# Dilated stage: ScalarE's conversions of weights and values kept behind the instruction written ahead of them, and two groups' weight loads issued by SyncE

## Chip, core and metric

The kernel runs on one core of one Trainium2 chip. The metric is the device time of one execution in microseconds; lower is better. Times are given as the median of several runs, and one further execution is recorded by the hardware profiler. All views shown here come from that one.

## What is computed

The kernel computes a trunk of two layers over 1024 tokens of width 1024: layer 0 mixes tokens by latent attention, layer 1 by dilated sliding-window attention, and each is followed by an MLP. The change touches the dilated attention alone:

```python
DIL_GROUPS = ((128, 1), (512, 4), (2048, 16))   # window, dilation
DIL_HEADS = 16
DIL_HEAD_DIM = 64

def dilated_mixer(h, pos, w_in, g_q, g_k, rel_bias, w_o):
    B, S, _ = h.shape
    proj = (h @ w_in).reshape(B, S, N_DIL_GROUPS, 3, DIL_HEADS, DIL_HEAD_DIM)
    outs, lses = [], []
    for gi, (window, dilation) in enumerate(DIL_GROUPS):
        q = rms_norm(proj[:, :, gi, 0], g_q[gi])
        k = rms_norm(proj[:, :, gi, 1], g_k[gi])
        v = proj[:, :, gi, 2]
        table = rel_bias[:, gi * DIL_HEADS:(gi + 1) * DIL_HEADS]
        o, lse = dilated_group(q, k, v, pos, table, window, dilation)
        outs.append(o)
        lses.append(lse)
    o_all = jnp.stack(outs, axis=0)
    wts = jax.nn.softmax(jnp.stack(lses, axis=0), axis=0)
    o = jnp.einsum('gbsh,gbshd->bshd', wts.astype(o_all.dtype), o_all)
    return o.reshape(B, S, DIL_HEADS * DIL_HEAD_DIM) @ w_o
```

Within a group, a query sees the keys of its own residue class within the window, with a bias by relative position; the three groups' outputs are merged by their softmax denominators.

## The kernel before

**Numbers in two parts.** A matrix product in float32 precision is made of three products of shorter numbers. Each operand is split into a high part (a ScalarE copy into the shorter type, line 121) and a low part (operand minus high part, line 122, mostly on VectorE); lines 414 to 416 multiply high by high, high by low and low by high. Values of v are split into three bf16 parts (lines 1815 to 1818), probabilities into two fp16 parts (lines 1923 and 1924).

**Steps of the dilated stage.** The values v of all groups are already projected and lie in HBM when `dil` (line 1749) starts; q and k are projected in it. It runs over a list of steps (line 2046): for each of the three groups 8 head pairs, for each pair 4 steps of two token tiles. Between two groups stands one step without a projection, in which the activations are permuted into the next group's token order (`permute`, line 2077: copies on ScalarE, VectorE and GpSimd); it begins already in the step before. Here these are called the turns. Group 0 fills the trace from 1669 to about 1953 us, group 1 from about 1987 to 2233, group 2 from about 2284 to 2552.

**One step n** writes, in this order:

- `fetch(n + 2)` (line 2054): if a head pair begins two steps on, its weights' loads, `dil_weights` (line 1542): two raw tiles `wqkr` of 512 KB, two DMAs of 256 KB each, issued by ScalarE;
- the parts of v that are due (`vtodo`, line 2063): for every second pair, which starts at step m, the loads `v_load` (SyncE) at step m − 4, and from step m − 2 on one call of `v_parts` in each step, five or four in all (line 1815 on ScalarE, 1816 on VectorE, 1817 and 1818 on GpSimd);
- at a turn, the permuting copies;
- `fetch_split(n + 1)` (line 2058): if a head pair begins at the next step, its weights' conversions, for each of the two raw tiles a high part `wqkh` on ScalarE and a low part `wqkl` on VectorE;
- `attend` (line 1898) for two earlier query tiles: the score products `pss` (line 1869), then for each tile the bias load `bt` (SyncE, line 1878), bias and row maximum (VectorE, 1883), the exponent's offset `dnb` and the exponentials (ScalarE, 1887 and 1889) and the two parts `ph` of the probabilities; then one DMA transpose `pT` of both (SyncE, line 1925);
- half of the projection `psproj`, the PE transposes `psq` of an earlier step (line 1844) with the split into `kT` (1848 and 1849), the other half of the projection;
- `av` (line 1928): the products `psav` with v of the tiles whose probabilities were transposed a step before;
- `qkstep` (line 1822): squares `dsq`, sums `dms`, the normalisation (line 112, Ln `drl`, and line 113, Exp `dry`, on ScalarE, then VectorE), and the scaled `qn`.

**What sets the order.** The program is not run as written. A planner, given the written program, puts each engine's instructions in an order of its own: with a modelled time for each, it lets an engine take the first written instruction whose inputs and buffer are there. So an instruction that depends on little, such as a load or a conversion of weights, can come out much earlier than it is written. On the chip every engine then runs its own list strictly in that order, and an instruction whose input is late holds up all that follow it in that list; DMA issues stand in the list of the engine that issues them. Two things bind the planner: `pinned` (line 203) keeps instructions of an engine in the order written, and `pin_from` (line 193) adds a dependence of each instruction on its engine's predecessor, without a wait on the chip, since one engine runs in order anyway. `pin_from` is used for TensorE in the dilated stage (line 2172), so there TensorE's order is the one written; ScalarE, VectorE, GpSimd and SyncE are the planner's.

**Buffers.** Weight tiles, raw values, merged outputs and permuted activations share one pool of 29 tiles (line 47); the planner gives a tile to a load when one is free. The converted values `vs` have 8 buffers of their own, the probabilities `ph` and `pT` two each, the bias tiles three.

Of the kernel before, what the change touches and what calls it, by code (L numbers as in the profile page):

```python
# [14 lines left out]
AF = mybir.ActivationFunctionType  # L15
# [26 lines left out]
class K:  # L42
# [150 lines left out]
    def pin_from(self, mark, engine=None):  # L193

        bb = self.nc.cur_bb.bb.instructions
        last = {}
        for n, i in enumerate(bb):
            prev, last[i.engine] = last.get(i.engine), i
            if n >= mark and prev is not None and engine in (None, i.engine):
                self.tc.add_manual_dep(i, prev.name, mybir.DependencyInfo(  # L200
                    mybir.DependencyClass.NoSync, mybir.DependencyReason.DATA), reason="pin_from")

    def pinned(self, ins):
        return self.tc.keep_in_program_order(ins)
# [1544 lines left out]
    def dil(self, at0, at1, tail, wqk, vd):  # L1749


        nc, a, tc = self.nc, self.a, self.tc
# [54 lines left out]
        def v_parts(raws, VS, t):  # L1807

            n = min(2, (9 if len(raws) == 3 else 8) - t)
            vs = D_("vs", (P, 2, 4, 192), BF16, 8)  # L1810
            p4 = raws[t // 4][:, t % 4 : t % 4 + n].rearrange("p i (h e) -> p (i h) e", e=64)
            v4 = vs[:, 0:n].rearrange("p i h e -> p (i h) e")
            r = self.T("vr")
            r4 = r.rearrange("p (i e) -> p i e", e=64)[:, 0 : 4 * n]
            nc.scalar.activation(v4[:, :, 0:64], p4, AF.Copy)
            nc.vector.tensor_tensor(r4, p4, v4[:, :, 0:64], op=ALU.subtract)
            nc.gpsimd.tensor_scalar(v4[:, :, 64:128], r4, 1.0, 1.0, op0=ALU.mult, op1=ALU.mult)
            nc.gpsimd.tensor_tensor(v4[:, :, 128:192], r4, v4[:, :, 64:128], op=ALU.subtract)
            for i in range(n):
                VS[t + i] = vs[:, i]  # L1820
# [195 lines left out]
        def emit(u, ths):  # L2016

            pr = u["pr"]
            if pr == 6:
                for k in range(2):  # L2020
                    for th in range(2):
                        O[k][th][3] = self.G(f"oT{k}", (P, 2, 512))
            for th in ths:
                ps = PS("psot")
                for i in range(4):
                    nc.tensor.transpose(ps[:, i * P : (i + 1) * P], u["U"][:, 4 * th + i, :], self.ident)
                if pr >= 6:
                    self.split(O[0][th][3][:, pr - 6, :], O[1][th][3][:, pr - 6, :], ps)
                else:
                    s_ = self.G("oT", (P, 2, 512))  # L2030
                    self.split(s_[:, 0, :], s_[:, 1, :], ps)
                    nc.scalar.dma_start(out=oTd[pr, th], in_=s_.bitcast(F32))
# [16 lines left out]
        loads, wts = {}, {}  # L2049
        mark = len(nc.cur_bb.bb.instructions)  # L2050
        end = max(n for n, x in enumerate(steps) if x is not None)
        firsts = {n: s for n, s in enumerate(steps) if s is not None and s[3] == 0}

        def fetch(n):
            if n in firsts:
                loads[n] = self.dil_weights(*firsts[n][1:3], eng=nc.scalar)

        def fetch_split(n):
            if n in firsts:
                wts[firsts[n][0:3]] = loads.pop(n)()  # L2060


        vtodo, VSs = {}, {}
        for n, (_, g, pr, _) in firsts.items():
            if pr % 2 == 0:
                VS = VSs[(g, pr // 2)] = {}
                VS["load"] = lambda g=g, c=pr // 2, VS=VS: VS.update(raws=v_load(g, c))
                vtodo.setdefault(n - 4, []).append(VS["load"])
                for t in range(0, 9 if g < 2 else 8, 2):
                    vtodo.setdefault(n - 2 + t // 2, []).append(lambda t=t, VS=VS: v_parts(VS["raws"], VS, t))  # L2070
                vtodo.setdefault(n - 2 + t // 2, []).append(lambda VS=VS: VS.pop("raws"))
# [35 lines left out]
        for n in sorted(vtodo):  # L2107
            if n < 0:
                for f in vtodo.pop(n):
                    f()  # L2110
        for n, step in enumerate(steps):
            fetch(n + 2)
            for f in vtodo.pop(n, ()):
                f()
# [11 lines left out]
            if step is not None:  # L2126
                kind, g, pr, tp = step
                w = wts[(kind, g, pr)]
                if tp == 0:
                    units[(g, pr)] = {"g": g, "pr": pr, "q": {}, "V": VSs[(g, pr // 2)],  # L2130
                                      "k": D_("kT", (P, 2, S + 512), F32R, 2), "U": self.G("U", (P, 8, P), F32)}
                u = units[(g, pr)]
            fetch_split(n + 1)
            transposed, scored = scored, attend(ready, n > end) if ready else []
            for u_, t_, _ in scored:
# [11 lines left out]
            if len(stk) > 1:  # L2147
                x = stk.pop(0)
# [200 lines left out]
```

## Time and profile before

| | |
|---|---|
| median of 3 runs | 3287.01 us (3286.89 to 3298.17) |
| the profiled execution | 3286.91 us |
| its span, from first to last instruction | 3285.1 us |
| mean granted TensorE clock | 0.983 |
| stretch 1660 to 2600 us, the dilated stage | 940 us |
| weight loads from ScalarE's queue | 92 DMAs of 256 KB |
| weight loads from SyncE's queue | 4 DMAs, written ahead of the stage |
| DMA transposes `pT` | 95 |

How to read the rows that follow. A row of busy time by stretch has the stretch, its length, then for TensorE's matmuls (PE), its weight loads into the array (PEld), VectorE (DVE), ScalarE (ACT) and GpSimd (POOL) the busy time and in parentheses the number of instructions, then the mean granted TensorE clock, the mean busy share of the 16 DMA engines and GB/s. That share can pass 1 in a short stretch, since a packet counts where it starts. A row of waits has the waiting instruction, what ended its wait, the total, how often, and the longest, in us. A row of the timeline has start, duration, engine (with a q where it is the queue that issues), line, operation, what is written and read, shape, count, and in brackets the engine's idle time ahead of it with what ended that. A row of groups has line, operation, shapes, count, then busy time, mean duration in ns, idle time ahead and what ended it. A row of the chain of waits has start and duration.

### The profile page before, as it was taken

What the parts mean: (1) busy time and instruction counts of PE and PEld (TensorE: products, weight loads), DVE (VectorE), ACT (ScalarE), POOL (GpSimd) and SP (SyncE); (2) the same over time, 40 slices, a digit from 0 to 9 for tenths busy, and PEclk for the clock granted to TensorE, in tenths of its full rate; (3) what the DMA queues carried; (4) which work ended last, traced back from release to release, by engine and by line L of the source; (5) the groups of instructions that cost most, each with busy time, mean ns of one, the idle gap of its engine ahead of it and who ended that gap; (6) DMA issues with size and microseconds to landing.
All of it is one profiled execution on the core that took longest, in us unless ns stands there. A gap on an engine that the chain in (4) does not pass through costs nothing. (4 is left out here: it accounts for less than half of the span.)

```text
span 3285.1 us, 50852 instructions
## 1 busy us (share of the span) xinstructions
PE 3143.2 (96%) x18034; PEld 2653.5 (81%) x18034; DVE 2406.5 (73%) x4272; ACT 1736.5 (53%) x3507; POOL 878.6 (27%) x1197
## 2 busy tenths in 40 slices
PE   6989999999999999899999989998999899999999
PEld 6877677778888788778889889997988788888887
DVE  5677777757987866787657777777888678778566
ACT  5547787745544433542246676667565355444342
POOL 7455555520111000001133334434333001110010
PEclk8999999999999999999999989998999999999999
DMA  5352233152654788536557877777677635438554
GB/s 189 123 182 91 94 94 100 57 185 87 211 188 162 283 246 281 171 103 210 194 141 167 171 169 171 184 169 160 152 174 180 198 98 203 148 142 321 204 192 129
DMA packets 538990, 552.31 MB, mean 168 GB/s; under 512 B 199493, under 2 KB 421106, under 8 KB 538730
## 3 DMA queue, kind: packets, MB, share of 16 engines
q1 hardware_dynamic: 452362, 418.88, 44.9%
q0 software_dynamic: 27360, 91.31, 7.5%
q10 hardware_dynamic: 59008, 38.81, 4.6%
q8 instruction: 144, 2.36, 0.3%
q14 instruction: 116, 0.95, 0.1%
HBM read 376.17 MB, written 132.62 MB: 155 GB/s over the span
## 5 line engine op out<-in xcount | busy, mean ns | idle before, releaser
L415 PE MATMUL psm<-dl,dh 128*128 128x512 f32 x896 | 351.2, 392 | 8.1 <-DVE dl L122 8.0
L414 PE MATMUL psm<-hf,wf 128*128 128x512 f32 x896 | 350.1, 391 | 2.6 <-ACT wf L121 2.6
L416 PE MATMUL psm<-dh,dl 128*128 128x512 f32 x896 | 350.1, 391 | 0.0
L415 PE MATMUL psm<-hf,wf 128*128 128x512 f32 x896 | 349.2, 390 | 0.0
L416 PE MATMUL psm<-hf,wf 128*128 128x512 f32 x896 | 347.3, 390 | 0.4 <-DVE wf L122 0.4
L414 PE MATMUL psm<-dh,dh 128*128 128x512 f32 x896 | 334.8, 391 | 4.7 <-ACT dh L121 4.7
L414 PE MATMUL psproj<-wqkh,hTp 128*128 128x256 f32 x1024 | 303.2, 296 | 0.0
L415 PE MATMUL psproj<-wqkl,hTp 128*128 128x256 f32 x1024 | 291.1, 284 | 0.0
L416 PE MATMUL psproj<-wqkh,hTp 128*128 128x256 f32 x1024 | 290.9, 284 | 0.0
L121 ACT ACTIVATE dh<-ufr 128x1024 fp32r<-128x1024 f32 x112 | 118.3, 1057 | 174.9 <-PE psm L416 51.4
L415 PEld LDWEIGHTS psm<-dl,dh 128*128 128x128 f32 x896 | 169.0, 189 | 46.0 <-DVE dl L122 11.3
L414 PEld LDWEIGHTS psproj<-wqkh,hTp 128*128 128x128 f32 x1024 | 197.6, 193 | 9.0 <-issue 0.9
L414 PEld LDWEIGHTS psm<-dh,dh 128*128 128x128 f32 x896 | 168.2, 188 | 42.2 <-ACT dh L121 7.0
L414 PEld LDWEIGHTS psm<-hf,wf 128*128 128x128 f32 x896 | 168.6, 188 | 40.3 <-ACT wf L121 5.5
L415 PEld LDWEIGHTS psproj<-wqkl,hTp 128*128 128x128 f32 x1024 | 197.9, 193 | 0.0
L416 PEld LDWEIGHTS psm<-hf,wf 128*128 128x128 f32 x896 | 168.5, 188 | 36.2 <-DVE wf L122 1.1
L416 PEld LDWEIGHTS psm<-dh,dl 128*128 128x128 f32 x896 | 169.1, 189 | 35.1
L416 PEld LDWEIGHTS psproj<-wqkh,hTp 128*128 128x128 f32 x1024 | 197.4, 193 | 0.0
L415 PEld LDWEIGHTS psm<-hf,wf 128*128 128x128 f32 x896 | 168.6, 188 | 34.6
L122 DVE TENSOR_TENSOR dl<-ufr,dh 128x1024 fp32r<-128x1024 f32 x112 | 136.5, 1219 | 78.1 <-ACT dh L121 58.3
L745 DVE TENSOR_REDUCE mx<-pmx 128x1 f32<-128x512 f32 x256 | 165.0, 681 | 27.6 <-PE pmx L743 27.4
L122 POOL TENSOR_TENSOR pl<-p,ph 128x1024 fp32r<-128x1024 f32 x58 | 141.3, 2436 | 136.1 <-ACT ph L121 125.9
(399 smaller groups left out, 8920.9 us busy)
## 6 DMA issues: line engine op xcount, KB each, us to landing
ufr<-uf SPq DMA_DIRECT2D x112, 512.0 KB
adaw<-in_ada_w SPq DMA_DIRECT2D x96, 512.0 KB
w2r<-in_mlp_w SPq DMA_DIRECT2D x96, 512.0 KB
w1r<-in_mlp_w SPq DMA_DIRECT2D x64, 512.0 KB
bt<-bias SPq DMA_DIRECT2D x128, 256.0 KB
wqkr<-in_dil_w_in ACTq DMA_DIRECT2D x92, 256.0 KB
qkv<-st SPq DMA_DIRECT2D x32, 512.0 KB
hraw<-qkv SPq DMA_DIRECT2D x32, 512.0 KB
```

Of the source, the lines that this page charges most:

```text
L121: nc.scalar.activation(hi, src, AF.Copy)
L122: (lo_eng or nc.vector).tensor_tensor(lo, src, hi.bitcast(F32), op=ALU.subtract)
L414: mm(out, lh, rh, start=first, stop=False)
L415: mm(out, lh, rl, start=False, stop=False)
L416: mm(out, ll, rh, start=False, stop=last)
L745: nc.vector.tensor_reduce(maxes[h][:, 2 * j + b : 2 * j + b + 1], ps, op=ALU.max, axis=AX.X)
```

## The change

A new method `held` calls a function that writes instructions, and makes each ScalarE instruction among them depend, for the planner alone, on the last ScalarE instruction written before the call. It is used for the conversion of v's values and for the conversions of the weights. In `held`, DMAs that ScalarE issues count as ScalarE instructions. The weights' loads of groups 0 and 1 are issued by SyncE instead of ScalarE; those of group 2 stay with ScalarE.

```diff
+    def held(self, emit):
+
+        bb = self.nc.cur_bb.bb.instructions
+        n = len(bb)
+        emit()
+        prev = next(x for x in reversed(bb[:n]) if x.engine == mybir.EngineType.Activation)
+        for i in bb[n:]:
+            if i.engine == prev.engine:
+                self.tc.add_manual_dep(i, prev.name, mybir.DependencyInfo(
+                    mybir.DependencyClass.NoSync, mybir.DependencyReason.DATA), reason="held")
...
-            nc.scalar.activation(v4[:, :, 0:64], p4, AF.Copy)
+            self.held(lambda: nc.scalar.activation(v4[:, :, 0:64], p4, AF.Copy))
...
         def fetch(n):
             if n in firsts:
-                loads[n] = self.dil_weights(*firsts[n][1:3], eng=nc.scalar)
+                loads[n] = self.dil_weights(*firsts[n][1:3], eng=nc.scalar if firsts[n][1] == 2 else nc.sync)
 
         def fetch_split(n):
             if n in firsts:
-                wts[firsts[n][0:3]] = loads.pop(n)()
+                self.held(lambda: wts.update({firsts[n][0:3]: loads.pop(n)()}))
```

## The prediction

> **What bounds the kernel now.** First the page: TensorE.
>
> ```profile
> span 3285.1 us, 50852 instructions
> PE 3143.2 (96%) x18034; PEld 2653.5 (81%) x18034; DVE 2406.5 (73%) x4272; ACT 1736.5 (53%) x3507; POOL 878.6 (27%) x1197
> ```
>
> TensorE is idle for 3285.1 − 3143.2 = 142 us, and only its idle or slowed time can be won. So next the busy time by stretches of the dilated stage: group 0, the turn to group 1, group 1, the turn to group 2, group 2, and then three short pieces of group 0.
>
> ```profile
> 1695.00:1953.00 258.00, 241.00 (x2219) 230.24 (x2216) 181.47 (x506) 165.90 (x482) 93.73 (x111) 0.97 0.78 166
> 1953.00:1987.00 34.00, 25.73 (x203) 22.70 (x202) 31.34 (x63) 26.59 (x58) 21.44 (x19) 0.80 0.69 159
> 1987.00:2233.00 246.00, 240.07 (x2261) 230.11 (x2258) 178.85 (x509) 158.47 (x471) 96.14 (x150) 1.00 0.79 177
> 2233.00:2284.00 51.00, 37.08 (x309) 34.06 (x308) 43.00 (x100) 39.06 (x104) 26.63 (x34) 0.80 0.69 152
> 2284.00:2552.00 268.00, 247.34 (x2206) 233.88 (x2208) 218.74 (x628) 152.81 (x520) 89.66 (x112) 0.99 0.72 170
> ...
> 1703.40:1720.00 16.60, 13.55 (x102) 12.81 (x101) 10.88 (x32) 9.05 (x26) 3.24 (x4) 0.79 0.94 174
> 1720.00:1742.00 22.00, 22.00 (x212) 21.21 (x213) 14.46 (x40) 13.36 (x40) 12.14 (x13) 1.00 0.46 108
> 1742.00:1752.90 10.90, 9.13 (x93) 8.54 (x89) 7.23 (x20) 7.60 (x19) 2.32 (x4) 1.00 1.14 246
> ```
>
> The idle time is 17.0, 8.3, 5.9, 13.9 and 20.7 us, 66 together. Within a group it is not spread out: 1720 to 1742 has none (DMA share 0.46), the pieces before and after it have 3.1 and 1.8 us, with DMA shares of 0.94 and 1.14. After the longer wait the granted clock is 0.79 too.
>
> What TensorE waited for, in group 0 and then in group 1:
>
> ```profile
> PE psav L1937 <- DMA pT<-ph: 14.0, 8, 3.3
> PE pss L1869 <- DVE kT L1849: 1.9, 2, 1.0
> PE pss L1869 <- ACT kT L1848: 1.0, 2, 0.5
> ```
>
> ```profile
> PE psav L1937 <- DMA pT<-ph: 3.3, 3, 1.4
> PE pss L1869 <- DVE kT L1849: 2.1, 3, 0.9
> PE pss L1869 <- ACT kT L1848: 0.6, 1, 0.6
> ```
>
> Mostly the probabilities' DMA transpose (pT). Why is it late? One pair change closely: the queues of SyncE, then ScalarE, then TensorE.
>
> ```profile
> 1733.41 1.98 SPq L1925 DMA_TRANSPOSE pT<-ph  x1
> 1735.66 1.35 SPq L1878 DMA_DIRECT2D bt<-bias  x2
> 1741.52 3.43 SPq L1925 DMA_TRANSPOSE pT<-ph  x1
> ```
>
> ```profile
> 1740.65 0.93 ACTq L1551 DMA_DIRECT2D wqkr<-in_dil_w_in  x2
> 1742.40 0.30 ACT L112 ACTIVATE drl<-dms,eps 128x8 f32<-128x8 f32 x1 [1.16 <-DVE dms L1829]
> 1742.40 0.37 ACTq L1551 DMA_DIRECT2D wqkr<-in_dil_w_in  x1
> ...
> 1742.85 0.59 ACTq L1551 DMA_DIRECT2D wqkr<-in_dil_w_in  x1
> 1743.93 0.64 ACT L1887 ACTIVATE dnb<-stat,ln 128x2 f32<-128x2 f32 x2 [0.89 <-DVE stat L1883]
> ...
> 1750.60 1.06 ACT L121 ACTIVATE wqkh<-wqkr 128x1024 fp32r<-128x1024 f32 x1 [1.59 <-DMA wqkr<-in_dil_w_in]
> ```
>
> ```profile
> 1750.77 0.26 PE L1937 MATMUL psav<-vs,pT 128*128 128x192 bf16 x1 [1.77 <-DMA pT<-ph]
> ```
>
> The four weight loads of a later head pair go out on ScalarE's queue within 1.3 us of the transpose, and both are slow: the transpose takes 1750.77 − 1741.52 = 9.25 us (its issue 3.43 instead of 1.98), the last load 7.75 (1742.85 to 1750.60), for which ScalarE stands 1.59 us at the head of its queue. A transpose with no load beside it, SyncE's row and the product that reads it without any idle time:
>
> ```profile
> 1798.60 1.93 SPq L1925 DMA_TRANSPOSE pT<-ph  x1
> ```
>
> ```profile
> 1803.62 0.26 PE L1937 MATMUL psav<-vs,pT 128*128 128x192 bf16 x1
> ```
>
> That one took 5.02 us at most. The four loads beside it cost a transpose 4.2 us or more.
>
> **The change, part by part.** (a) 60 weight loads (7 pairs of group 0, 8 of group 1, four each) leave ScalarE's queue for SyncE's, where they stand in one row with the transposes and the bias loads; group 2's 32 stay. (b) No conversion of weights, in all three groups, is issued ahead of the ScalarE instruction written before it, which is as a rule the last of the step before last's normalisation. (c) The same for the conversions of v (line 1815), which stand up to five in as many steps from two ahead of every second pair. No arithmetic is added or removed.
>
> *(a), the transposes.* At stake are the transpose waits, less the longest of group 0, which comes just ahead of the turn at 1953, where the copies for group 1 crowd the engines:
>
> ```profile
> 1942.55 0.26 PE L1937 MATMUL psav<-vs,pT 128*128 128x192 bf16 x1 [3.31 <-DMA pT<-ph]
> ```
>
> This leaves 14.0 − 3.3 in group 0 and 3.3 in group 1, 14.0 us. To this comes the slowed clock: in group 0 the mean is 0.97, so up to 0.03 × 258 = 7.7 us are lost, and I put two thirds of it, 5, down to waits at loads. Together 19 us. On SyncE the loads find a hole: the bias issue ends at 1735.66 + 1.35 = 1737.01, and the queue stands until 1741.52, 4.5 us, in each step. Four issues of 0.37 to 0.59 us, some 1.9 us, fit, and their packets are out before the transpose's; placed behind the transpose they have the whole next step. Bounds: 0 (they stay beside it) to −19. I take 70%, −13, nearer the full sum since one queue can't issue beside itself; the rest are loads that get their buffer late and push a transpose.
>
> *(a), the queues.* ScalarE's is rid of 60 issues of about (0.93 + 0.37 + 0.59)/4 = 0.47 us, 28 us in all. Above they fall into its 1.16 us wait for dms and under its running instructions; worth 0 on the path, and −1 of each four's 1.9 us at most if that cover is not there. SyncE pays the same in its 4.5 us holes; the price where a hole is missed is 1.9 us of delay for the transpose and the bias loads behind it, for which the attention product and the scores wait.
>
> *(b), the standing ScalarE.* The view of waits gives for group 0, group 1, and v in group 2:
>
> ```profile
> ACT wqkh L121 <- DMA wqkr<-in_dil_w_in: 13.5, 7, 2.7
> ```
>
> ```profile
> ACT wqkh L121 <- DMA wqkr<-in_dil_w_in: 7.6, 8, 1.6
> ```
>
> ```profile
> ACT vs L1815 <- DMA vraw<-v: 10.6, 4, 4.0
> ```
>
> Held back by a step or more, the conversions find their data landed. Behind them on ScalarE stand the exponentials, the ph and the kT copies; what reached TensorE of it are the kT rows: 2.9 in group 0 and 2.7 in group 1, 5.6 us. Bounds 0 to −5.6; I take −5. At the two turns the second pair's conversions now fall in between the permuting copies; moved three steps on, they leave VectorE (31.34 busy of 34.00) two subtractions. Bounds 0 to −8.3 at the first and −13.9 at the second (all their idle time); I take −1 each, nearest to the 0.3 to 1.0 us of the kT waits, as VectorE stays full with the copies. In group 2, −1 of the 10.6 us of standing, bounds −4 to +4, since VectorE is 218.74/268 = 82% busy there.
>
> *(b), the crowding.* The price of one conversion of weights and of one of v (ScalarE's, VectorE's):
>
> ```profile
> L121 ACT ACTIVATE wqkh<-wqkr 128x1024 fp32r<-128x1024 f32 x46 | 48.4, 1052 | 44.7 <-DMA wqkr<-in_dil_w_in 25.0 <-PE psv L415 15.1 <-DVE wqkl L122 3.6
> L122 DVE TENSOR_TENSOR wqkl<-wqkr,wqkh 128x1024 fp32r<-128x1024 f32 x46 | 60.9, 1324 | 23.3 <-ACT wqkh L121 21.9 <-ACT dsq L1828 1.0
> ...
> L1816 DVE TENSOR_TENSOR vr<-vraw,vs 128x512 f32<-128x512 f32 x48 | 33.5, 703 | 0.7 <-DMA v<-vz 0.7
> ```
>
> The two halves of a pair now fall into one step: 2.10 us of ScalarE and 2.65 of VectorE. A step without gap takes some 8.4 us, 1703.40 − 1695.00, and in 1720 to 1742 the rest needs 13.36/22 × 8.4 = 5.1 of ScalarE and 14.46/22 × 8.4 = 5.5 of VectorE. Sums 7.2 and 8.2: it just fits, and an added v conversion (0.7 on VectorE) brings that to 8.9, 0.5 over, in every second pair. Bounds 0 (the conversions go into ScalarE's waits for VectorE) to 2.10 for each of 23 changes. I take 0.5 for half of the 15 in groups 0 and 1, +4 rounded up, nearer the low end by that sum, and count group 2's in its own bounds.
>
> *Sum*: −13 − 5 − 2 − 1 + 4 = −17 us, from the profiled execution's 3286.91 us (span 3285.1 and 1.8 around it), which is 0.1 under the median of 3287.01: 3270 us.
>
> A rule speaks against (a): the Trainium skill's "DMA: Bandwidth & Descriptors", "Issuing engines are not separate DMA queues", has all issuers' transfers interleave on the same 16 DMA engines, so that another issuer only changes the issue time. By it (a)'s −13 would be 0 and the sum −4, which is rival B's time. The rows agree that the two interleave; that they must meet at all they don't show.
>
> **The rivals.**
>
> *B: the transposes stay late.* Loads ready just before a transpose are ahead of it in one row and must drain first. Interleaved they delay it by 4.2 us above; ahead of it in one row the delay is the same or more, with 1.9 us of issue on top at worst. Then (a) is worth 0 and the sum is −4: 3283 us. For it: today the loads come out beside the transposes in the piece shown; against: the 4.5 us hole. The same page's "Queues, rings and completion order" says that descriptors of a row are consumed in ring order while rows take turns packet by packet, which is what B would need.
>
> *C: the change does not do what it says.* The order holds a conversion only behind its predecessor, which the planner may also issue early, so conversions still stand for their data, and waits only move: −2 us, 3285.
>
> *D: slower, the crowded step.* The conversions go ahead of the step's exponentials, and 2.10 us of delay go through ph into the transpose. Place: ScalarE, right behind the normalisation's Exp, at each of 23 changes. At 2.10 each 48 us, less the 21 of the gains: +27, 3314; at two thirds of it +11, 3298. It decides from 21/23 = 0.9 us a change on. For it: VectorE's 8.2 to 8.9 of 8.4; against: ScalarE has holes within every step, 1.16 us ahead of the normalisation (1742.40) and 0.89 us ahead of the scores' offsets (1743.93).
>
> *E: the turns gain too.* If the 22 us idle at the turns and their clock of 0.80 ease by half, −15 more: 3255.
>
> **How the numbers follow.** The forecast 0.44, B 0.18, C 0.07, D 0.22, E 0.09. A difference under 0.5%, 16.4 us, can't be told from none here, and the forecast of −17 lies on that bound: its own range is 3256 to 3280, of which I count 0.28 as faster and 0.16 as same. B counts 0.03 as faster and 0.15 as same, C all as same, D 0.15 as slower and 0.07 as same, E all as faster. That makes faster 0.40, same 0.45, slower 0.15. The range takes in B and C, E, and the lower part of D: 3248 to 3300.
>
> **What would show it.** (a) is right if the transpose waits of groups 0 and 1 fall from 17.3 to under 7 us, transpose issues stay near 2 us at pair changes, and the clock of group 0 is above 0.98. (b) is right if ScalarE's waits for the weights nearly vanish (13.5 and 7.6) and with them those for kT. B shows as transposes still late, with SyncE's load issues right ahead of them; D as conversions back to back ahead of dnb and later ph; late weights as waits of the projections for wqkl. I am wrong if the saving comes from outside 1690 to 2560, if the idle time of group 2 grows by more than 4 us, or if the order elsewhere in the kernel is recast.

## The result, and the profile after

The changed kernel takes 3261.76 us (median of 6 runs, 3256.55 to 3266.25), the kernel before in the runs beside it 3286.95 us (6 runs, 3282.86 to 3298.17): a ratio of 0.9919 with an interval from 0.9902 to 0.9936, 25 us or 0.8% less. Forecast were 3270 us and a range of 3248 to 3300. The profiled execution of the changed kernel took 3266.25 us, the longest of its six runs, so the two profiles differ by 20.7 us only; the sums below are made against those 20.7.

All lines have moved by 11 in the part read here: the product `psav` is line 1948, the scores `pss` 1880, the split into `kT` 1859 and 1860, the transpose 1936, a weight load 1562, a conversion of v 1826.

The page of the changed kernel, busy time and then one of the DMA queues (packets, MB, share of 16 engines):

```profile
span 3264.5 us, 50798 instructions
PE 3145.6 (96%) x18034; PEld 2660.3 (81%) x18034; DVE 2404.1 (74%) x4272; ACT 1735.4 (53%) x3507; POOL 892.6 (27%) x1197
...
q10 hardware_dynamic: 27328, 23.07, 2.7%
```

TensorE does the same 18034 matmuls in the same busy time (3145.6 for 3143.2 us), and the span is 20.6 us shorter: what went is idle time. In the page of before this queue had 38.81 MB, so 15.7 MB changed queues, which is the 60 loads of 256 KB.

Where it went is read from a table of pieces with the same work: group 0 from its first projection to its last, then the turn, which here reaches to the second step's projections of the next group, then that group to its last projection, and so on; group 2 is taken to just ahead of the output projection. The numbers of matmuls agree (2426, some 140, 2425, 141, 2449), so the lengths can be compared directly. Columns as in the prediction's first windows. Before:

```profile
1668.84:1952.58 283.74, 266.50 (x2426) 254.90 (x2425) 197.51 (x539) 178.17 (x508) 107.23 (x129) 0.98 0.76 164
1952.58:1978.66 26.08, 18.60 (x141) 15.89 (x139) 26.05 (x46) 21.78 (x43) 15.79 (x13) 0.74 0.62 159
1978.66:2247.08 268.42, 259.76 (x2425) 248.72 (x2424) 195.44 (x558) 176.66 (x526) 108.73 (x167) 0.99 0.79 174
2247.08:2275.38 28.30, 16.99 (x141) 15.19 (x138) 25.51 (x49) 21.01 (x49) 15.47 (x19) 0.70 0.65 163
2275.38:2582.22 306.84, 283.78 (x2449) 265.00 (x2448) 240.77 (x700) 167.91 (x577) 95.56 (x120) 0.98 0.70 169
```

After:

```profile
1671.10:1936.63 265.53, 262.09 (x2426) 250.99 (x2425) 198.59 (x539) 174.93 (x503) 111.49 (x129) 0.99 0.75 176
1936.63:1965.75 29.12, 18.61 (x140) 16.35 (x139) 26.10 (x49) 21.28 (x45) 15.16 (x13) 0.74 0.60 142
1965.75:2229.62 263.87, 259.92 (x2425) 250.16 (x2424) 194.09 (x554) 177.00 (x526) 115.08 (x168) 0.98 0.80 178
2229.62:2254.82 25.20, 18.26 (x141) 16.11 (x139) 22.09 (x50) 18.95 (x47) 14.17 (x19) 0.73 0.59 147
2254.82:2561.80 306.98, 288.06 (x2449) 271.64 (x2448) 240.13 (x700) 170.56 (x580) 100.42 (x117) 0.96 0.73 171
```

| piece | length, before to after | difference | TensorE idle (length minus busy) |
|---|---|---|---|
| up to the first projection of group 0 | 1668.84 to 1671.10 | +2.3 | |
| group 0 | 283.74 to 265.53 | −18.2 | 17.2 to 3.4 |
| first turn | 26.08 to 29.12 | +3.0 | 7.5 to 10.5 |
| group 1 | 268.42 to 263.87 | −4.6 | 8.7 to 4.0 |
| second turn | 28.30 to 25.20 | −3.1 | 11.3 to 6.9 |
| group 2 | 306.84 to 306.98 | +0.1 | 23.1 to 18.9 |
| the rest | 702.9 to 702.7 | −0.2 | |

Groups 0 and 1 won 22.8 us, the two turns nothing together, and all else lost 2.2. In group 0, 13.8 us are idle time and 4.4 a shorter busy time, at a granted clock of 0.99 instead of 0.98. Group 2 shows the opposite: 4.1 us less idle, and 4.3 us more busy at 0.96 instead of 0.98.

What TensorE still waits for in the changed kernel, first in group 0 (1671 to 1937 us) and then in group 1 (1966 to 2230):

```profile
PE psav L1948 <- DMA pT<-ph: 2.3, 3, 1.9
PE pss L1880 <- DVE kT L1860: 0.7, 3, 0.4
```

```profile
PE psav L1948 <- DMA pT<-ph: 4.0, 1, 4.0
```

The waits for the transposes are 6.3 us; in the same two pieces of before they were 14.0 and 6.0, 20.0 together (the prediction's 17.3 is over shorter windows). In the two turns they went the other way, from 8.5 to 10.5. The two long ones that are left (1.9 and 4.0) stand shortly ahead of the turns, at transposes with weight loads 0.7 to 1.4 us ahead of them (1919.59 and 2208.84; at the latter these are group 2's, from ScalarE's queue). Between 1695 and 1925 us 0.4 us are left. ScalarE's waits for the weights, 13.5 and 7.6 before, have no row any more in these stretches.

The same pair change that the prediction took apart, in the changed kernel: SyncE's queue, then ScalarE, then the product that reads the transpose of 1746.27.

```profile
1738.21 1.78 SPq L1936 DMA_TRANSPOSE pT<-ph  x1
...
1741.21 3.20 SPq L1562 DMA_DIRECT2D wqkr<-in_dil_w_in  x4
...
1746.27 4.16 SPq L1936 DMA_TRANSPOSE pT<-ph  x1
...
1756.33 1.92 SPq L1936 DMA_TRANSPOSE pT<-ph  x1
```

```profile
1758.12 1.05 ACT L121 ACTIVATE wqkh<-wqkr 128x1024 fp32r<-128x1024 f32 x1
1759.08 0.46 ACT L1898 ACTIVATE dnb<-stat,ln 128x2 f32<-128x2 f32 x2
1759.45 1.04 ACT L121 ACTIVATE wqkh<-wqkr 128x1024 fp32r<-128x1024 f32 x1
```

```profile
1753.93 0.26 PE L1948 MATMUL psav<-vs,pT 128*128 128x192 bf16 x1
```

The four loads start 3.0 to 5.7 us behind one transpose and 5.1 to 2.4 ahead of the next, where before they lay from 0.9 ahead to 1.3 behind. The next transpose has a long issue all the same, 4.16 us, but its product starts at 1753.93 with no idle time in brackets: it had 7.66 us and took no more. Before, the product came 9.25 us behind its transpose and had waited 1.77, so it would have started 7.48 behind. That is the slack of this step: about 7.5 us from the start of the transpose, which 9 overrun and 7 do not. It is not the same in every step: ahead of the turn the product at 1926.56 came 6.97 us behind its transpose (1919.59) and had waited 1.91. The conversions start 13.7 us behind the end of the loads' issue (1758.12 for 1744.41) and wait for nothing; `dnb` runs between the two.

### The profile page after: what moved, and what is told of

Same layout as the page of the kernel before. It is cut to its first block, busy times and chain, and to the rows that moved or that the text cites. A ratio compares the mean times of both kernels' runs of the same rounds, so it can differ in the third digit from the quotient of the medians.

```text
span 3264.5 us, 50798 instructions
## 1 busy us (share of the span) xinstructions
PE 3145.6 (96%) x18034; PEld 2660.3 (81%) x18034; DVE 2404.1 (74%) x4272; ACT 1735.4 (53%) x3507; POOL 892.6 (27%) x1197
## 4 chain that ended last, share of the span: by engine, by line
PE 48%; DVE 5%; DMA 5%; issue 2%; POOL 1%; ACT 1%; SPq 0%; ACTq 0%; DVEq 0%; POOLq 0%
PE psm L426 7%; PE psm L427 7%; PE psm L425 7%; PE psproj L425 4%; PE psproj L426 4%; PE psproj L427 4%; PE pss L1880 2%; DMA pT<-ph 2%; PE psv L426 2%; PE psv L427 2%; PE psv L425 2%; PE psav L1948 1%; PE psy L425 1%; PE psy L427 1%; PE psy L426 1%
## 5 line engine op out<-in xcount | busy, mean ns | idle before, releaser
L425 PE MATMUL psproj<-wqkh,hTp 128*128 128x256 f32 x1024 | 307.4, 300 | 0.0
L427 PE MATMUL psproj<-wqkh,hTp 128*128 128x256 f32 x1024 | 294.5, 288 | 0.0
L425 PEld LDWEIGHTS psproj<-wqkh,hTp 128*128 128x128 f32 x1024 | 201.9, 197 | 9.3 <-issue 1.6
L426 PEld LDWEIGHTS psm<-dl,dh 128*128 128x128 f32 x896 | 169.6, 189 | 45.3 <-DVE dl L122 10.1
L427 PEld LDWEIGHTS psproj<-wqkh,hTp 128*128 128x128 f32 x1024 | 201.3, 197 | 0.0
L1846 POOL TENSOR_TENSOR qn<-qn,dgain 128x256 f32<-128x256 f32 x96 | 92.1, 959 | 382.1 <-DVE qn L1844 303.0
```

The lines of the kernel that those rows point to most:

```text
L425: mm(out, lh, rh, start=first, stop=False)
L426: mm(out, lh, rl, start=False, stop=False)
L427: mm(out, ll, rh, start=False, stop=last)
L1846: nc.gpsimd.tensor_tensor(qq, qq, gain[:, g : g + 1, :].unsqueeze(1).broadcast_to([P, 2, 2, 64]), op=ALU.mult)
```

## The experiments

Each was made from the changed kernel; ratios are to the kernel before in the runs beside it.

**e1: the loads alone.** Both calls of `held` are taken out, so that only the issuer of the loads differs from before.

```diff
-            self.held(lambda: nc.scalar.activation(v4[:, :, 0:64], p4, AF.Copy))
+            nc.scalar.activation(v4[:, :, 0:64], p4, AF.Copy)
...
-                self.held(lambda: wts.update({firsts[n][0:3]: loads.pop(n)()}))
+                wts[firsts[n][0:3]] = loads.pop(n)()
```

> The loads of groups 0 and 1 on SyncE, no conversion held. Theory (the transposes gain, the conversions add the kT part): the transpose waits of groups 0 and 1 fall from 17.3 to under 5 us, ScalarE still stands for weights it converts early, and the kernel gains 12 to 20 of the 25 us, 3267 to 3275. Rival (the held order is what gains, the queue is of no account): under 5 us gained, 3282 or more.

Measured: 3284.25 us (12 runs) beside 3287.95 of the kernel before (23 runs), 0.999 (0.9981 to 1.0): 3.7 us less, and 6 at the lower end of the interval, where 12 to 20 had been expected. At the pair change taken apart above SyncE's list is that of the changed kernel, loads at 1741.16 and a transpose at 1746.22. But ScalarE:

```profile
1746.56 1.06 ACT L121 ACTIVATE wqkh<-wqkr 128x1024 fp32r<-128x1024 f32 x1 [2.56 <-DMA wqkr<-in_dil_w_in]
1748.51 1.06 ACT L121 ACTIVATE wqkh<-wqkr 128x1024 fp32r<-128x1024 f32 x1 [0.89 <-DMA wqkr<-in_dil_w_in]
```

SyncE's next transposes and the product that reads the second of them:

```profile
1746.22 4.62 SPq L1936 DMA_TRANSPOSE pT<-ph  x1
...
1758.46 1.79 SPq L1936 DMA_TRANSPOSE pT<-ph  x1
```

```profile
1764.17 0.26 PE L1948 MATMUL psav<-vs,pT 128*128 128x192 bf16 x1 [1.51 <-DMA pT<-ph]
```

The planner puts the conversions right behind the loads, wherever these go, and ScalarE stands 3.45 us at its head for data that has just been ordered. The exponentials are late, the next transpose is issued 12.2 us behind the last instead of 10.1, and TensorE waits for it a step later than before. The wait is again booked to the transpose, though this one took under 6 us: it was started late. In the steady stretch of group 0 (1695 to 1925 us) ScalarE's standing grows to 15.6 us, in that of group 1 (1985 to 2205) from 7.6 to 15.5:

```profile
ACT wqkh L121 <- DMA wqkr<-in_dil_w_in: 15.6, 10, 2.6
```

```profile
ACT wqkh L121 <- DMA wqkr<-in_dil_w_in: 15.5, 9, 3.4
```

The longest wait of this kernel, though, lies at the first turn, and it has another cause. SyncE's queue, the product behind the transpose, and the busy time of the turn:

```profile
1940.01 16.50 SPq L1889 DMA_DIRECT2D bt<-bias  x4
1956.62 3.25 SPq L1936 DMA_TRANSPOSE pT<-ph  x1
```

```profile
1961.74 0.34 PE L1948 MATMUL psav<-vs,pT 128*128 128x192 bf16 x1 [11.74 <-DMA pT<-ph]
```

```profile
1944.52:1977.75 33.23, 16.29 (x141) 14.44 (x138) 25.21 (x46) 21.45 (x43) 15.49 (x15) 0.74 0.51 124
```

In this kernel four bias loads stand ahead of the transpose in SyncE's list, and SyncE stands 14.2 us at the third of them, until VectorE's bias step (line 1894) has run at 1955.8. In the changed kernel the transpose of this turn (1940.63) is ahead of the two bias loads (1947.56). The last part of `ph` is written by 1951.97, so 4.65 of the 11.74 us are SyncE's list. The rest is `ph` itself, which is complete 7.5 us behind the last projection of the group, and 3.4 us behind it in the kernel before; why was not found. So taking `held` out changed more than the time of the conversions: the planner ordered SyncE's list at the turn anew.

**e2: the order alone.** `held` stays, all loads go back to ScalarE's queue.

```diff
-                loads[n] = self.dil_weights(*firsts[n][1:3], eng=nc.scalar if firsts[n][1] == 2 else nc.sync)
+                loads[n] = self.dil_weights(*firsts[n][1:3], eng=nc.scalar)
```

> All conversions held, all loads still on ScalarE's queue. Theory: the loads still meet the transposes, whose waits in groups 0 and 1 stay above 10 us; only the standing ScalarE and the kT waits go: 3 to 8 us gained, 3279 to 3284. Rival (held order gains): transposes are late only because ScalarE stood ahead of the probabilities, so their waits fall under 6 us and 15 us or more are gained.

Measured: 3281.96 us, 0.9983 (0.9973 to 0.9993), 6 us less. ScalarE waits no more for weights, but the loads are again beside a transpose (ScalarE's queue, SyncE's, the product):

```profile
1743.48 0.93 ACTq L1562 DMA_DIRECT2D wqkr<-in_dil_w_in  x2
...
1745.26 0.37 ACTq L1562 DMA_DIRECT2D wqkr<-in_dil_w_in  x1
```

```profile
1744.59 3.31 SPq L1936 DMA_TRANSPOSE pT<-ph  x1
```

```profile
1754.45 0.26 PE L1948 MATMUL psav<-vs,pT 128*128 128x192 bf16 x1 [2.59 <-DMA pT<-ph]
```

The product starts 9.86 us behind the transpose, after a wait of 2.59. From 1695 to 1925 us the waits for transposes are 8.9 us here, from 1985 to 2205 us 7.8, where the kernel before had 10.7 and 4.1 in the same stretches.

So the totals don't add up: 3.7 and 6.0 us alone, 25 together. The pieces, cut as above, say where (lengths in us):

| profile | group 0 | first turn | group 1 | second turn | both groups, against before | both turns, against before |
|---|---|---|---|---|---|---|
| before | 283.7 | 26.1 | 268.4 | 28.3 | | |
| changed | 265.5 | 29.1 | 263.9 | 25.2 | −22.8 | −0.1 |
| changed once more (e9) | 264.7 | 29.5 | 261.6 | 27.0 | −25.8 | +2.1 |
| e1, loads alone | 273.7 | 33.2 | 265.2 | 29.4 | −13.3 | +8.3 |
| e2, order alone | 277.8 | 27.1 | 271.6 | 27.6 | −2.7 | +0.4 |

In groups 0 and 1 the loads alone win 13.3 us and the order alone 2.7, and both together 7 to 10 us beyond that sum. There were two faults at the pair changes. Loads beside a transpose make this transpose late; conversions right behind the loads make the next one late. With either of them left TensorE still waits there. The other part of the difference are e1's turns, which give 8.3 us back. These are single profiles: the two of the changed kernel differ by up to 2.3 us in a piece, e1's is the fastest of its 12 runs, and e2's is 4 us above its median, so that the 6 us of e2's runs are not seen whole in its pieces. The gain in the groups is clear of this: e3, e4, e5, e8, e9, e10 and e12 below, in which the loads keep their distance and the weights' conversions are held, take 524 to 530 us for the two groups, the kernel before 552.

**e3, e4 and e8: how much of the change is needed.** e3 sends group 2's loads by SyncE as well; e4 leaves group 2's conversions of weights to the planner; e8 does both.

```diff
-                loads[n] = self.dil_weights(*firsts[n][1:3], eng=nc.scalar if firsts[n][1] == 2 else nc.sync)
+                loads[n] = self.dil_weights(*firsts[n][1:3], eng=nc.sync)
```

```diff
-                self.held(lambda: wts.update({firsts[n][0:3]: loads.pop(n)()}))
+                f = lambda: wts.update({firsts[n][0:3]: loads.pop(n)()})
+                self.held(f) if firsts[n][1] < 2 else f()
```

> As the changed kernel, with group 2's loads on SyncE too. Theory (SyncE has a hole after each transpose, in group 2 as well): transposes in group 2 are no later than in the changed kernel, within 5 us of it, 3257 to 3267. Rival (group 2 has shorter steps and other transfers on SyncE, the loads push its transposes): 5 to 15 us slower than the changed kernel.

> As the changed kernel, but the weight conversions of group 2 are not held. In the changed kernel group 2 shows a wait of 2.1 to 2.4 us at four pair changes, where before it had waits of 0.3 to 1.2 us. Theory (two conversions in one step are too much for VectorE in group 2): these waits go and 3 to 8 us are gained on the changed kernel, 3254 to 3259. Rival (the waits have another cause, v's conversions or the merge): within 3 us of the changed kernel.

> All three groups' loads on SyncE, v's conversions held everywhere, weights' conversions held in groups 0 and 1 only. If the two single steps (all loads on SyncE; group 2 not held) each win a little in group 2 and their wins add up, 3255 to 3259; if loads on SyncE need the held order, as in groups 0 and 1, group 2 loses 3 to 8 us: 3264 to 3270.

Measured: e3 3262.05 us, 0.9923 (0.991 to 0.9937); e4 3260.86, 0.9918 (0.9905 to 0.9931); e8 3265.83, 0.9918 (0.9903 to 0.9932). None can be told from the changed kernel, and the 3 to 8 us that e4 was expected to gain did not come: the gain needs nothing in group 2. What `held` does there shows in the profile all the same. The waits of group 2 in the changed kernel:

```profile
PE pss L1880 <- DVE kT L1860: 7.3, 5, 2.3
...
PE pss L1880 <- DVE U L1950: 3.9, 1, 3.9
```

The same in e4, and its stretch of group 2:

```profile
PE pss L1880 <- DVE qn L1844: 8.2, 1, 8.2
...
PE pss L1880 <- DVE kT L1860: 2.9, 6, 0.9
```

```profile
2248.37:2552.34 303.97, 282.87 (x2449) 265.01 (x2448) 240.00 (x699) 168.53 (x578) 95.68 (x120) 0.98 0.72 173
```

With the conversions kept late the scores wait for `kT` five times, up to 2.3 us; left to the planner, they don't (0.9 at most), but one wait of 8.2 us stands at the end of the group, where the changed kernel has 3.9. In sum e4 is idle 21.1 us there and the changed kernel 18.9, yet e4's group is 3.0 us shorter, since the same 2449 matmuls take 282.87 us at a clock of 0.98 and 288.06 at 0.96. Three microseconds in one profile of each are not told apart by the runs.

**e5 and e12: v's conversions.** e5 leaves v's conversions to the planner. In e12 they are free too, but a held conversion of weights is bound to the last ScalarE instruction that is not a conversion of v.

```diff
-            self.held(lambda: nc.scalar.activation(v4[:, :, 0:64], p4, AF.Copy))
+            nc.scalar.activation(v4[:, :, 0:64], p4, AF.Copy)
```

```diff
+        self.free = set()
...
-        prev = next(x for x in reversed(bb[:n]) if x.engine == mybir.EngineType.Activation)
+        prev = next(x for x in reversed(bb[:n]) if x.engine == mybir.EngineType.Activation and x.name not in self.free)
...
-            self.held(lambda: nc.scalar.activation(v4[:, :, 0:64], p4, AF.Copy))
+            nc.scalar.activation(v4[:, :, 0:64], p4, AF.Copy)
+            self.free.add(nc.cur_bb.bb.instructions[-1].name)
```

> As the changed kernel, but the conversions of v are not held. Theory (the weights' conversions need the order, since their loads are the ones that went to another queue; v's loads were on SyncE all along): within 5 us of the changed kernel's 3262. Rival (v's conversions stood for their loads as long as the weights', 10.6 us in group 2 alone): 5 to 12 us of the gain is lost.

> As the run in which v's conversions are not held (e5), but the weights' conversions are bound past v's: to the last ScalarE instruction written before that is no conversion of v, in general the normalisation's Exp. In e5 ScalarE stood for weights again at every second pair, since there the instruction written just ahead is a conversion of v that itself comes early. Theory (e5 lost its 5 us because the weights' hold was loose there): ScalarE stands for weights no longer, and the ratio to before is that of the changed kernel, 0.991 to 0.9925. Rival (v's own early conversions cost it): ratio 0.993 or more, with ScalarE standing for v.

Measured: e5 3269.83 us, 0.9932 (0.9919 to 0.9945); e12 3263.0, 0.9921 (0.9909 to 0.9934). By its ratio e5 gives 3 to 4 us of the gain back, with an interval that overlaps those of the changed kernel and of e12, so that a loss is not shown. From 1695 to 1925 us its ScalarE stands for weights again:

```profile
ACT wqkh L121 <- DMA wqkr<-in_dil_w_in: 6.5, 3, 3.6
ACT vs L1826 <- DMA vraw<-v: 5.0, 3, 2.9
```

e12 has no row for the weights there, and the same 5.0 us for v, and is as fast as the changed kernel. So v's own standing costs nothing that can be seen here. ScalarE stands for weights in e5 because at every second pair the instruction written ahead of a conversion of weights is one of v's: where it is free to go early, it holds nothing back. Whether this standing costs time stays open. In e5's profile groups 0 and 1 with their turns take 582.7 us, in the changed kernel's two 583.7 and 582.8.

**e6 and e7: ScalarE's queue, loads held back.** All loads go by ScalarE, and are bound in the planner's order as well: in e6 behind the first `dnb` of their step, in e7 behind the ScalarE instruction written ahead of them. The idea was to keep the queue and change only the time.

```diff
-                loads[n] = self.dil_weights(*firsts[n][1:3], eng=nc.scalar if firsts[n][1] == 2 else nc.sync)
+                pend.append(lambda: loads.update({n: self.dil_weights(*firsts[n][1:3], eng=nc.scalar)}))
...
             nc.scalar.activation(nb, stat[:, g, t, 0, 2 * pr : 2 * pr + 2], AF.Identity, scale=-1.0, bias=ln14)
+            while pend:
+                self.held(pend.pop(0))
```

```diff
-                loads[n] = self.dil_weights(*firsts[n][1:3], eng=nc.scalar if firsts[n][1] == 2 else nc.sync)
+                self.held(lambda: loads.update({n: self.dil_weights(*firsts[n][1:3], eng=nc.scalar)}))
```

> All loads on ScalarE's queue, all conversions held, and each pair's four loads held behind the first row-maximum offset (dnb) of the step in which they are written, which is some 2.4 us behind a transpose's issue and 6 us ahead of the next. Theory (what counts is when the loads come, not whose queue they are in): transposes land within 7 us as in the changed kernel; the four issues of 0.5 us now stand ahead of the exponentials, which may give 0.5 to 1 us back at each change; 8 to 20 us gained on before, 3267 to 3279. Rival (two queues at once are what is slow): transposes next to loads still take 8.5 us or more, and under 5 us are gained.

> All loads on ScalarE's queue, loads and conversions held, so that the loads come behind the normalisation's Exp instead of right behind the squares: about 1 to 1.5 us behind a transpose's issue instead of within a microsecond ahead of it. Theory (time of the loads): transposes take 6.5 to 9 us, between the 9 to 10 with the loads ahead of them and the undisturbed 5; 5 to 12 us gained on before. Rival (the queue): as without this hold, 8.5 to 10 us a transpose and 5 us gained.

Measured: e6 3303.04 us, 1.0042 (1.003 to 1.0055), e7 3308.47 us, 1.0061 (1.0048 to 1.0075): both slower than the kernel before, where gains of 8 to 20 and of 5 to 12 us were expected. In groups 0 and 1 no transpose with loads close to it landed more than 6.8 us behind its start by the trace's semaphore events, so these were on time, but now the loads are late. e7's ScalarE at one pair change:

```profile
1783.42 2.67 ACTq L1562 DMA_DIRECT2D wqkr<-in_dil_w_in  x4
...
1793.53 1.04 ACT L121 ACTIVATE wqkh<-wqkr 128x1024 fp32r<-128x1024 f32 x1
```

In group 1 (1985 to 2205 us) the projections of e7 wait for the low parts, and in group 2 (2284 to 2530 us) its scores wait for `kT`:

```profile
PE psproj L426 <- DVE wqkl L122: 4.4, 4, 1.3
```

```profile
PE pss L1880 <- DVE kT L1860: 20.8, 11, 5.0
```

Loads held back by most of a step push the conversions into the last moment, and the slowdown is largest in group 2. By pieces e7's groups 0 and 1 are 15.0 and 3.6 us shorter than before, its turns 8.9 and 7.0 longer, and group 2 to its last projection 21.8 longer. As totals these two don't tell whether the queue matters, since the loads also moved too far.

**e9: the changed kernel once more**, without an edit, beside e10 and e11.

> The changed kernel itself, unaltered, as the measure for the other runs beside it: 3262, within 4 us, if before stands at 3287 in this set; otherwise the same distance of 20 to 30 us below it.

Measured: 3264.08 us, 0.9922 (0.9908 to 0.9936), the first result again; its group 2 has the same five waits for `kT`, 7.2 us.

**e10 and e11: ScalarE's queue, a step earlier.** The loads of groups 0 and 1 are written one step earlier and go by ScalarE; in e10 they are bound behind the instruction written ahead of them, the normalisation's Exp, in e11 behind the first `dnb` (with the lines of e6). Group 2's loads and all conversions are as in the changed kernel.

```diff
-                loads[n] = self.dil_weights(*firsts[n][1:3], eng=nc.scalar if firsts[n][1] == 2 else nc.sync)
+                f = lambda: loads.update({n: self.dil_weights(*firsts[n][1:3], eng=nc.scalar)})
+                self.held(f) if firsts[n][1] < 2 else f()
...
-            fetch(n + 2)
+            for m in (n + 3, n + 2):
+                if m in firsts and (firsts[m][1] < 2) == (m == n + 3):
+                    fetch(m)
```

> Groups 0 and 1 with their loads on ScalarE's queue again, but written one step earlier and held behind the normalisation's Exp; all conversions held; group 2 as in the changed kernel. The loads then come some 6 us ahead of the next transpose and two steps ahead of their conversions. Theory (the time of the loads counts, not the queue): transposes under 7 us, no late low parts, within 6 us of the changed kernel. Rival (SyncE's queue itself is worth something): over 10 us slower than the changed kernel, with transposes or conversions late in groups 0 and 1.

> As the run beside it, with the loads held behind the step's first row-maximum offset instead, so that their four issues (2 us) stand ahead of the exponentials. Theory: the same save for those issues, 0 to 2 us at each of 15 changes: 5 to 20 us slower than the run beside it, transposes themselves under 7 us. Rival (issues hide under ScalarE's waits there too): within 4 us of it.

Measured: e10 3269.07 us, 0.9945 (0.9931 to 0.9958); e11 3279.51 us, 0.9976 (0.9965 to 0.9986). One pair change of e10, SyncE, ScalarE's queue, TensorE:

```profile
1772.88 1.84 SPq L1936 DMA_TRANSPOSE pT<-ph  x1
```

```profile
1774.34 4.55 ACTq L1562 DMA_DIRECT2D wqkr<-in_dil_w_in  x4
```

```profile
1780.45 0.26 PE L1948 MATMUL psav<-vs,pT 128*128 128x192 bf16 x1
```

And of e11:

```profile
1775.85 4.43 SPq L1938 DMA_TRANSPOSE pT<-ph  x1
```

```profile
1777.23 3.73 ACTq L1562 DMA_DIRECT2D wqkr<-in_dil_w_in  x4
```

```profile
1786.27 0.26 PE L1950 MATMUL psav<-vs,pT 128*128 128x192 bf16 x1 [3.69 <-DMA pT<-ph]
```

In e10 the product follows 7.57 us behind the transpose and waits for nothing; over 1695 to 1925 us the waits for transposes are 0.2 us, as small as in the changed kernel. e10's groups 0 and 1, each with its turn, and its group 2:

```profile
1673.38:1969.03 295.65, 278.14 (x2564) 265.87 (x2562) 217.76 (x582) 193.80 (x544) 127.38 (x141) 0.97 0.74 169
1969.03:2255.21 286.18, 274.65 (x2563) 262.69 (x2561) 221.28 (x608) 194.66 (x575) 129.99 (x186) 0.98 0.79 182
2255.21:2565.76 310.55, 285.94 (x2450) 269.38 (x2449) 239.78 (x700) 170.38 (x580) 100.03 (x117) 0.96 0.72 169
```

The first two take 295.65 and 286.18 us, where the changed kernel has 294.65 (265.53 + 29.12) and 289.07. So in groups 0 and 1 SyncE's row is not needed, as far as one profile shows: loads that come at the right time do the same from ScalarE's. e10's median is 5 us above that of e9; in its profile 3.6 us lie in group 2 (310.55 for 306.98), and why is not settled. e11 is some 10 us slower than e10, within the 5 to 20 expected, but not by the issues alone as supposed there: its transposes, which were to be on time, are not. In e11 the loads lie much as in e10, 1.4 us behind the start of a transpose for 1.5, and yet three transposes of group 0 (1775.85, 1848.71 and 1929.94) take over 10 us: at that distance it can go either way. What decides there was not found.

## Why the prediction was right, and where not

**The direction and the place were right.** The saving lies between 1690 and 2560 us, in groups 0 and 1, by the two mechanisms named: transposes that meet the loads, and a ScalarE that stands for weights. Of the signs that were set, the transposes' waits (6.3 us, under 7, outside the turns), group 0's clock (0.99, above 0.98), ScalarE's waits for weights (gone) and those for `kT` in groups 0 and 1 (0.7 us for 5.6) came out.

**The sum was too small: 17 for 25 us, and for 20.7 in the profiled execution.** By terms, against the profiled pieces:

- *Transposes −13, ScalarE −5, crowding +4* make −14 in groups 0 and 1; measured were −22.8. At stake were 19 + 5.6 = 24.6 us, and nearly all of it went. The 70% for the transposes fits the loads alone (−13.3 in e1) and was too careful for both together: the loads found their place behind the previous transpose at the steady pair changes, and of the waits 0.4 us were left from 1695 to 1925. The crowding was the worst-sized term: the two conversions at 1758.12 and 1759.45 lie in one step with `dnb` between them, and TensorE's waits for `kT` in group 0 are 0.7 us. It is seen in group 2 alone, by comparison with e4: five waits for `kT` of up to 2.3 us and a lower clock, against a longer wait at the end of the group.
- *The turns −2*: +3.0 and −3.1, nothing together. *Group 2 −1*: +0.1. The 2.3 us by which the stage starts later were not foreseen; over the profiles of all these kernels the start lies between 1668.84 and 1675.5 us, and its cause stays open.

**The weak step is the adding up.** (a) and (b) were priced as two terms, as if neither changed the other. In groups 0 and 1 (a) alone comes out at its price, 13.3 us for 13 in e1's profile, and (b) alone under it, 2.7 for 5 in e2's, and both together win 22.8. The sum had no term for that. The reason stood in the rows of before: the planner places a conversion as soon as its load is expected, so earlier loads bring earlier conversions, and ScalarE's standing goes with them (from 21.1 to 31.1 us in e1, both stretches together). Nor had it a term for the order in which SyncE's list comes out at the turns, where e1 gives 8.3 us back, 4.65 of them in that list. That the changed kernel was spared this is luck as far as the prediction goes, which did not look at that order. Together the two faults had 24.6 us at stake in these groups, and nearly all of it came only when both were gone.

**A sign was wrong.** Transposes' issues were to stay near 2 us at pair changes; in the changed kernel they are 4.16 us at 1746.27, and still the product doesn't wait. A long issue was read as lateness because in the piece of before the two came together. Lateness is the time from the transpose's start to its product, held against the slack, about 7.5 us at that step.

**The rivals.** B (transposes stay late in SyncE's row) fell: the loads are issued ahead of the transpose in one row, as B had it, but 2 to 5 us ahead and not right ahead, and 0.4 us of waits are left between 1695 and 1925 us. Close ahead of the first turn, where two loads are 0.7 and 1.2 us ahead of the transpose of 1919.59 in its own row, its product does wait, 1.9 us. The rule beside B, the Trainium skill's "DMA: Bandwidth & Descriptors", section "Issuing engines are not separate DMA queues", says that another issuer changes the issue time alone. e10 agrees as far as groups 0 and 1 go: the queue is indifferent (295.65 and 286.18 us for 294.65 and 289.07). The time at which the loads go out is not, and the change of the issuer was the way by which the planner moved it; so the −4 worked out beside the rule fell with B. C (the planner may issue the predecessor early too) fell for the changed kernel, but e5 shows it at work: with v's conversions free, the weights' are held behind something that is itself early, and ScalarE stands 6.5 us, at no cost that the runs show. D (slower, by late conversions) did not happen here; e6 and e7 show a relative, at 0.4% and 0.6%, once the loads themselves are late. E (the turns gain) fell, with nothing in sum.

## What to carry to other kernels

Two faults that end in the same wait don't have prices of their own: try each alone before adding them, and read each half by pieces of equal work and not by its total. Here the halves gave 3.7 and 6 us and the whole 25, but the first half had won 13 in the groups and lost 8 at the turns, where the planner's new order put a transpose behind bias loads that had to wait. A planner that issues an instruction as soon as its input is expected follows a moved load with everything that hangs on it, so moving a load and holding its consumer belong together. For a transfer on the path, measure the slack from its start to its consumer, and put bulk loads where they stay clear of that stretch; whose queue issues them matters less.

## What the runs showed of the hardware that was not expected

In groups 0 and 1, four loads of 256 KB that start within about 1 us of a DMA transpose go with 9.3 (before) and 9.9 us (e2) from its start to its product; started 2.4 to 5.1 us ahead of it they leave it within 7.66 us, though they are ahead of it in its own row. By the transposes' semaphore events this holds over both groups: in the kernel before twelve transposes whose first load starts from 0.9 us ahead of them to 0.9 behind landed 7.0 to 10.3 us behind their start; in the changed kernel eleven with all four loads 2.0 to 5.1 us ahead landed in 5.3 to 7.6. It does not hold for group 2, whose transposes have issues of 1.24 us: in the kernel before two of them, with a first load 0 and 0.2 us behind their start, landed in 5.2 and 4.2 us. At 1.4 to 1.5 us behind a transpose's start both outcomes occur, 7.6 us or less in e10 and 10.4 in e11. And the length of the issue of a transpose says little by itself: 4.16 us with a product that didn't wait, as well as 4.43 with one that waited 3.69.
